# A two-layer hybrid diffusion trunk on one core: mixer parameters loaded at the stage's head, eight modulation halves beside each FFN, all mixer weight splits on VectorE

## The chip, the cores and the metric

The kernel runs on one core of a Trainium2 chip. It is one launch. The metric is the device time of the launch in microseconds, as the median of several runs; beside it stands one profiled execution, from which every row below comes. The engines are TensorE (PE; its weight loads are listed apart as PEld), VectorE (DVE), ScalarE (ACT), GpSimd (POOL) and SyncE (SP), which here only issues DMAs.

## What is computed

384 tokens (128 context tokens and 256 latent ones) of width 1024 pass through two layers, all in float32. The reference, cut to what matters here:

```python
def trunk_layer(x, cond, lp, l, cache):
    mod = silu(cond) @ lp['w_ada'] + lp['b_ada']      # w_ada: 1024 x (9*1024), per layer
    mod = mod.reshape(cond.shape[0], 9, 1, 1024)      # nine vectors, for two conds
    h = rms_norm(x, norm_g[0]) * (1 + mod[:, 1]) + mod[:, 0]
    x = x + 0.5 * mod[:, 2] * swiglu(h, w_gate[0], w_up[0], w_down[0])   # 1024 -> 2816 -> 1024
    h = rms_norm(x, norm_g[1]) * (1 + mod[:, 4]) + mod[:, 3]
    x = x + mod[:, 5] * token_mix(h, lp, l, cache)
    h = rms_norm(x, norm_g[2]) * (1 + mod[:, 7]) + mod[:, 6]
    return x + 0.5 * mod[:, 8] * swiglu(h, w_gate[1], w_up[1], w_down[1])

def token_mix(h, lp, l, cache):
    proj = h @ lp['w_in']            # queries, keys, values, gates of four mixers; 4*1024 merge logits
    out_a = gated_delta(...)         # A: DeltaNet, a triangular solve in every chunk of 64
    lam = exp(sum(lam_p[0]*lam_p[1])) - exp(sum(lam_p[2]*lam_p[3])) + lam_init   # da_lambda
    out_b = diff_attention(rope(rms(b_q)), rope(rms(b_k)), b_v, lam)   # B: two softmaxes, lam between
    out_c = mlstm(...)               # C
    out_d = retention(...)           # D, decay from ret_decay_logit
    y = sum(sigmoid(merge_logits[m]) * (out[m] @ lp['w_branch'][m]) for m in range(4))
    return y @ lp['w_out']
```

It also returns the new states of the four mixers and the new keys and values.

## The kernel before

**Layout.** Tokens lie in the free dimension (384 wide), features in eight blocks of 128 partitions. Each weight tile (128x8x128, or 128x2x512 in the down-projections) comes by DMA as `raw` (1 MB, two tiles, three buffers, issued by SP). `split_unit` then makes two parts of it: `whi`, a cast on ScalarE (L168), and `wlo`, the rest, a subtraction on VectorE or GpSimd (L172). There are three buffers of each part. A product takes three matmuls per block: L185, L186 (both with `whi`) and L187 (with `wlo`).

**Stages.** Each layer runs FFN1 (`ffn`: 22 gate and up tiles, then the down-projection in two halves `dg` of 11 splits each), a norm, `mixers`, a norm, and FFN2. In `mixers` the branches come in the order retention, mLSTM, DeltaNet's first part, attention, DeltaNet's last part; `merge` computes gates (`mg`, branches 3, 2, 1, 0) and branch products (`pb`) and is interleaved with attention and DeltaNet. DeltaNet's solve is a chain of 31 rows in turn on VectorE (the `aR` loop: multiply L1335, reduce L1337, each row longer than the one before).

**Order.** A scheduler with a cost model sets the order of the instructions of every engine. The order is fixed when the kernel is built; at run time each engine works its own list from the top and waits on semaphores. A tile that waits for a buffer, or a VectorE instruction that waits for a DMA, holds all that stands behind it on its engine.

**Modulation vectors.** A vector `mod` of a layer is a product of two conditions with 1024x1024 of `w_ada`. It is made in one of two ways. On TensorE (`ada`): two halves, each with 16 matmul records that write `arow` (L261), then four small transposes `acol` (L271). On VectorE (`ada_beside`): per half four loads `braw` of 512 KB (two buffers, L300) and 20 VectorE instructions, two scalings (L315), 14 multiply-adds (L317), two transposes (L323) and two reductions (L324); a generator hands them out in steps of two instructions, ten steps per half, one step after each split that VectorE does in `ffn`. At the end of an FFN the rest of the generator is run out.

**Splits in `mixers`.** In the projections the second tile of each load is split on GpSimd (`lo_eng`), and so are the gates and branch weights of branches 3, 2 and 1 (`POOLM`). With ten others (units 2 and 3 after a norm) these are 98 splits on GpSimd. GpSimd also adds the branch results to `y` (L1487).

**Small parameters.** The gate biases `gb`, `al`, the decay logits `lg`, the rotary table `rope`, the norm weights `bgn` and the `da_lambda` product `blp` are loaded where they are used. `blp` (L1109) is issued at the head of attention, its first VectorE instruction is L1112; `nlam` and `rg` follow from these.

Of the kernel before, what the change touches and what calls it, by code (L numbers as in the profile page):

```python
# [8 lines left out]
F32 = mybir.dt.float32  # L9
# [32 lines left out]
POOLM = (3, 2, 1)  # L42
# [74 lines left out]
class Trunk:  # L117
# [431 lines left out]
    def ffn_body(self, l, i, jobs, beside, nxt):  # L549
# [40 lines left out]
        for dg in range(2):  # L590
            acc = [self.mmps(name="pd") for _ in range(4)]
            units = []
            for f in range(0, KF, 4):
# [4 lines left out]
                for q in range(0, nf, 2):  # L598
                    w = split(raw[:, q:q + 2], [128, 2, 512])
# [115 lines left out]
    def gate_stage(self, l, keep, p):  # L715
# [3 lines left out]
        gb = p.tile([128, 4, 8], F32, tag="gb", name="gb")  # L719
        nc.vector.memset(gb[:, 0], 0.0)  # L720
        al = p.tile([128, 8], F32, tag="al", name="al")
        for dst, nm in ((gb[:, 1], "dn_dt_bias"), (gb[:, 2], "ml_i_bias"), (gb[:, 3], "ml_f_bias"), (al, "dn_a_log")):
            nc.sync.dma_start(dst, I[nm][l].rearrange("d h -> (d h)").unsqueeze(0).to_broadcast([128, 8]))
# [17 lines left out]
        nc.scalar.activation(out=al, in_=al, func=AF.Exp)  # L741
# [115 lines left out]
    def mix_ret(self, l, p):  # L857
        nc, I = self.nc, self.I
        lg = p.tile([128, 12], F32, name="lg")
        nc.sync.dma_start(lg[:, 0:8], I["ret_decay_logit"][l].rearrange("d h -> (d h)").unsqueeze(0).to_broadcast([128, 8]))  # L860
        nc.vector.tensor_copy(lg[:, 8:12], self.prm[l][:, R_RT:R_RT + 4])
        nc.vector.tensor_scalar_mul(lg, lg, -1.0)
        self.softplus(lg, [128, 12])
        nc.vector.tensor_scalar_mul(lg, lg, -1.0)
# [226 lines left out]
    def mix_attn(self, l, p):  # L1091
        nc, I = self.nc, self.I
        lam0 = 0.8 - 0.6 * math.exp(-0.3 * l)
        rope = p.tile([128, 2, 2, 32], F32, name="rope")
        nc.sync.dma_start(rope, I["rope"])
        gn = p.tile([128, 2, 32], F32, name="bgn")
        nc.sync.dma_start(gn[:, 0], I["da_qn_g"][l:l + 1].to_broadcast([128, 32]))
        nc.sync.dma_start(gn[:, 1], I["da_kn_g"][l:l + 1].to_broadcast([128, 32]))

        rg = p.tile([128, 2, 2, 2, 32], F32, name="brg")  # L1100
        for b in range(2):
            nc.gpsimd.tensor_tensor(rg[:, b, 0], gn, rope[:, b, 0].unsqueeze(1).to_broadcast([128, 2, 32]), op=ALU.mult)
            for a in range(2):
                sv, gv, ov = (t.rearrange("p i (g a e) -> p i g a e", a=2, e=8) for t in (
                    rope[:, b, 1].unsqueeze(1).to_broadcast([128, 2, 32]), gn, rg[:, b, 1]))
                for i in range(2):
                    nc.gpsimd.tensor_tensor(ov[:, i, :, a], gv[:, i, :, 1 - a], sv[:, i, :, a], op=ALU.mult)
# [3 lines left out]
        lam = p.tile([128, 2], F32, name="blam")  # L1111
# [505 lines left out]
```

## Time and profile before

| | |
|---|---|
| median of three runs | 2138.11 us (2131.19 to 2139.86) |
| the profiled execution, its own time | 2140.96 us |
| span of the profile | 2139.2 us |
| mean granted TensorE clock | 0.978 of full speed |
| busy: PE, DVE, ACT, POOL | 96%, 69%, 39%, 22% |

How to read it: the span is what lies between the first and the last recorded instruction; the profiled execution's own time is 1.8 us longer. A stretch of the span, from one time to another, can be asked for each engine's busy time; a busy TensorE is then compared with the length of the stretch. In the lists of instructions a bracket at the end names how long the engine stood idle just before that row, and what ended the idle time. The chain that ended last goes back from the last instruction to what released each one.

### The profile page before, as it was taken

Reading aid. Unit: us, or ns where it says so; the run is one execution under the profiler, and the core shown is the slowest. Engines: PE = TensorE matmul, PEld = TensorE weight load, DVE = VectorE, ACT = ScalarE, POOL = GpSimd, SP = SyncE. Lnnn points to the kernel's source line nnn. Section 1 sums busy time; section 2 is a strip of 40 time slices with the busy share of each in tenths; the row PEclk is TensorE's granted clock in tenths of the full one; section 3 lists DMA queues with packets and bytes.
Section 4 is the critical chain, followed back from the end, with each engine's and each line's share of the span. In section 5 each row is a group of like instructions: output and inputs, shape, how many; then the busy total and the mean of one; then the engine's idle time right before and its main releaser. Section 6 shows DMA issues by size and latency. Waiting matters only on the chain.

```text
span 2139.2 us, 31932 instructions
## 1 busy us (share of the span) xinstructions
PE 2062.1 (96%) x12450; PEld 1992.0 (93%) x12450; DVE 1469.3 (69%) x2716; ACT 842.9 (39%) x1514; POOL 466.2 (22%) x375
## 2 busy tenths in 40 slices
PE   7999999988899999999999999999888999999999
PEld 5889999888789999999999999999877999999999
DVE  4867678678955578776778776678699445795433
ACT  3533335453343245333344332363533423463322
POOL 3000014434354252000120000243243722500000
PEclk8999999999899999999999999999998999999999
DMA  9775545434142355565467554444332423454432
GB/s 312 266 266 171 172 139 173 132 97 121 52 123 70 111 187 171 185 186 178 148 221 260 169 177 168 144 127 138 99 99 77 116 72 129 148 167 128 135 123 79
DMA packets 280566, 322.75 MB, mean 151 GB/s; under 512 B 42784, under 2 KB 214368, under 8 KB 280160
## 3 DMA queue, kind: packets, MB, share of 16 engines
q1 hardware_dynamic: 280144, 320.46, 47.7%
q8 instruction: 98, 1.61, 0.3%
q14 instruction: 52, 0.43, 0.1%
q10 hardware_dynamic: 272, 0.26, 0.0%
HBM read 313.00 MB, written 7.69 MB: 150 GB/s over the span
## 4 chain that ended last, share of the span: by engine, by line
PE 83%; DVE 13%; DMA 2%; ACT 1%; issue 1%; SPq 0%; DVEq 0%; ACTq 0%
PE pg L185 6%; PE pd L185 6%; PE pg L186 6%; PE pd L186 6%; PE pd L187 6%; PE pg L187 6%; PE pu L187 6%; PE pu L185 6%; PE pu L186 6%; PE mg L187 3%; PE mg L185 3%; PE mg L186 3%; DVE aR L1335 2%; PE mm L185 1%; PE mm L186 1%; PE mx L1389 1%
## 5 line engine op out<-in xcount | busy, mean ns | idle before, releaser
L168 ACT CAST whi<-raw 128x1024 fp32r<-128x1024 f32 x422 | 442.6, 1050 | 880.8 <-PE pd L186 212.9
L172 DVE TENSOR_TENSOR wlo<-raw,whi 128x1024 fp32r<-128x1024 f32 x324 | 401.3, 1239 | 304.1 <-ACT whi L168 298.8
L172 POOL TENSOR_TENSOR wlo<-raw,whi 128x1024 fp32r<-128x1024 f32 x98 | 246.4, 2518 | 331.6 <-ACT whi L168 304.9
L386 POOL TENSOR_SCALAR xg<-xT,gs 128x128 f32<-128x128 f32 (+1 forms) x96 | 92.8, 982 | 798.3 <-DVE xT L538 775.7
L185 PE MATMUL pd<-hh,whi 128*128 128x384 f32 x704 | 237.6, 337 | 0.0
L186 PE MATMUL pd<-hl,whi 128*128 128x384 f32 x704 | 237.3, 337 | 0.0
L187 PE MATMUL pd<-hh,wlo 128*128 128x384 f32 x704 | 234.8, 337 | 0.0
L317 DVE SCALAR_TENSOR_TENSOR acc<-braw,cond,acc 128x512 f32<-128x512 f32 x280 | 198.7, 749 | 0.2 <-DMA braw<-in_w_ada 0.2
L185 PE MATMUL pg<-hhi,whi 128*128 128x384 f32 x536 | 180.2, 336 | 0.0
L186 PE MATMUL pg<-hlo,whi 128*128 128x384 f32 x536 | 179.4, 335 | 0.0
L187 PE MATMUL pg<-hhi,wlo 128*128 128x384 f32 x536 | 179.3, 334 | 0.0
L185 PE MATMUL pu<-hhi,whi 128*128 128x384 f32 x536 | 179.1, 334 | 0.0
L187 PE MATMUL pu<-hhi,wlo 128*128 128x384 f32 x536 | 179.1, 334 | 0.0
L186 PE MATMUL pu<-hlo,whi 128*128 128x384 f32 x536 | 179.1, 334 | 0.0
L185 PE MATMUL mg<-hhi,whi 128*128 128x384 f32 x512 | 178.0, 348 | 0.0
L186 PE MATMUL mg<-hlo,whi 128*128 128x384 f32 x512 | 177.3, 346 | 0.0
L187 PE MATMUL mg<-hhi,wlo 128*128 128x384 f32 x512 | 175.5, 344 | 0.9 <-DVE wlo L172 0.9
L186 PEld LDWEIGHTS pd<-hl,whi 128*128 128x128 f32 x704 | 132.3, 188 | 0.1
L185 PEld LDWEIGHTS pd<-hh,whi 128*128 128x128 f32 x704 | 132.3, 188 | 0.1
L187 PEld LDWEIGHTS pd<-hh,wlo 128*128 128x128 f32 x704 | 132.1, 188 | 0.0
L185 PEld LDWEIGHTS pg<-hhi,whi 128*128 128x128 f32 x536 | 100.6, 188 | 3.6 <-ACT hh L581 3.4
L186 PEld LDWEIGHTS pg<-hlo,whi 128*128 128x128 f32 x536 | 100.7, 188 | 1.7 <-issue 1.7
(417 smaller groups left out, 4629.5 us busy)
## 6 DMA issues: line engine op xcount, KB each, us to landing
raw<-in_w_in SPq DMA_DIRECT2D x62, 1024.0 KB
raw<-in_ffn_w_gate SPq DMA_DIRECT2D x44, 1024.0 KB
raw<-in_ffn_w_up SPq DMA_DIRECT2D x44, 1024.0 KB
braw<-in_w_ada SPq DMA_DIRECT2D x80, 512.0 KB
raw<-in_ffn_w_down SPq DMA_DIRECT2D x40, 1024.0 KB
araw<-in_w_ada SPq DMA_DIRECT2D x32, 1024.0 KB
raw<-in_w_branch SPq DMA_DIRECT2D x16, 512.0 KB
raw<-in_w_out SPq DMA_DIRECT2D x8, 1024.0 KB
```

What stands on the lines that cost most here:

```text
L168: nc.scalar.copy(hi, src)
L172: self.last_split = (eng or nc.vector).tensor_tensor(lo, src, hi.bitcast(F32), op=ALU.subtract)
L185: nc.tensor.matmul(ps, w[0], x[0], start=start, stop=False)
L186: nc.tensor.matmul(ps, w[0], x[1], start=False, stop=False)
L187: self.last_mm = nc.tensor.matmul(ps, w[1], x[0], start=False, stop=stop)
L317: nc.vector.scalar_tensor_tensor(acc[s], raw[:, g], c, acc[s], op0=ALU.mult, op1=ALU.add)
L386: self.nc.gpsimd.tensor_scalar(xg[kk][:, a:e], self.xT[:, kk, a:e], gs[:, s, kk:kk + 1], None, op0=ALU.mult)
L1335: nc.vector.tensor_tensor(pr, X[:, 0:r, 0:r].rearrange("p k c -> p c k"), M[:, r, 0:r].unsqueeze(1).to_broadcast([112, r, r]), op=ALU.mult)
L1389: nc.tensor.matmul(ps[:, 64 * h:64 * h + 64], Z[d][:, b, h], x[:, 64 * h:64 * h + 64], start=(h == 0), stop=(h == 3))
```

## The change

It does three things.

1. Each of the FFNs (layer, i) = (0,0), (0,1) and (1,0) has eight halves of modulation vectors beside it, where it had six; vectors 4 of layer 0 and 3 and 4 of layer 1 go from `ada` to `ada_beside`. A split in the down-projection hands out two steps where it handed out one.
2. `mixer_parameters`, called first in `mixers`, loads and computes the small parameters. They live in the stage's pool, `blp` and `rope` in the ring of temporaries.
3. `lo_eng` and `POOLM` are gone: 88 of the 98 splits on GpSimd go to VectorE, 44 in each layer.

```diff
-POOLM = (3, 2, 1)
...
-        def split(src, shape):
+        def split(src, shape, n=1):
             w = self.split_unit(src, shape)
             if self.last_split.ins.engine == mybir.EngineType.DVE:
                 with self.after(self.last_split):
-                    next(beside, None)
+                    for _ in range(n):
+                        next(beside, None)
             return w
...
-                    w = split(raw[:, q:q + 2], [128, 2, 512])
+                    w = split(raw[:, q:q + 2], [128, 2, 512], 2)
...
-    def lo_eng(self, m):
-        return self.nc.gpsimd if m else self.nc.vector
...
-            w = self.split_unit(raw[:, :, 128 * m:128 * m + 128], [128, KD, 128], self.lo_eng(m))
+            w = self.split_unit(raw[:, :, 128 * m:128 * m + 128], [128, KD, 128])
...
-        lp = p.tmp([128, 2, 2, 32], "blp")
-        nc.sync.dma_start(lp, I["da_lambda"][l].rearrange("a d -> (a d)").unsqueeze(0).to_broadcast([128, 128]).rearrange(
-            "p (a b d) -> p a b d", a=2, b=2))
...
-            eng = nc.gpsimd if m in POOLM else nc.vector
...
-            w = self.split_unit(cur["g"][:, :, 128 * q:128 * q + 128], [128, KD, 128], eng)
+            w = self.split_unit(cur["g"][:, :, 128 * q:128 * q + 128], [128, KD, 128])
...
+    def mixer_parameters(self, l):
...
+        lp = self.ring.tmp([128, 2, 2, 32], "blp")
+        lam = bp.tile([128, 4], F32, name="blam", bufs=1)
+        rope = self.ring.tmp([128, 2, 2, 32], "rope")
...
+        for dst, nm in ((self.gb[:, 1], "dn_dt_bias"), (self.gb[:, 2], "ml_i_bias"), (self.gb[:, 3], "ml_f_bias"),
+                        (self.al, "dn_a_log"), (self.lg[:, 0:8], "ret_decay_logit")):
+            nc.sync.dma_start(dst, I[nm][l].rearrange("d h -> (d h)").unsqueeze(0).to_broadcast([128, 8]))
...
     def mixers(self, l):
         nc = self.nc
         with self.pool("bp") as self.bp:
+            self.mixer_parameters(l)
             xs = self.dr.tile([128, KD, T], F32, tag="xs", name="xs", bufs=1)
...
-                mods = {(0, 0): (0, (2, 3, 4)), (0, 1): (0, (8,)), (1, 0): (1, (3, 4)), (1, 1): None}
-                slow = {(0, 0): ((0, 5), (0, 6), (0, 7)), (0, 1): ((1, 0), (1, 1), (1, 2)), (1, 0): ((1, 5), (1, 6), (1, 7)),
-                        (1, 1): ((1, 8),)}
+                mods = {(0, 0): (0, (2, 3)), (0, 1): (0, (8,))}
+                slow = {(0, 0): ((0, m) for m in (4, 5, 6, 7)), (0, 1): ((1, m) for m in (0, 1, 2, 3)),
+                        (1, 0): ((1, m) for m in (4, 5, 6, 7)), (1, 1): ((1, 8),)}
```

What stands where, as the two builds give it. Lines of the kernel after are those of its own file.

VectorE in the down-projection of FFN1 of layer 0, before (`braw`, `acc`, `cond`: load, sum and condition of a modulation half):

```order
L172 TENSOR_TENSOR wlo<-raw,whi 128x1024
L317 SCALAR_TENSOR_TENSOR acc<-braw,cond,acc 128x512 x2
L172 TENSOR_TENSOR wlo<-raw,whi 128x1024
L317 SCALAR_TENSOR_TENSOR acc<-braw,cond,acc 128x512 x2
L172 TENSOR_TENSOR wlo<-raw,whi 128x1024
L317 SCALAR_TENSOR_TENSOR acc<-braw,cond,acc 128x512 x2
```

The same place after:

```order
L171 TENSOR_TENSOR wlo<-raw,whi 128x1024
L316 SCALAR_TENSOR_TENSOR acc<-braw,cond,acc 128x512 x4
L171 TENSOR_TENSOR wlo<-raw,whi 128x1024
L316 SCALAR_TENSOR_TENSOR acc<-braw,cond,acc 128x512 x4
L171 TENSOR_TENSOR wlo<-raw,whi 128x1024
```

Between two splits there are four instructions of the modulation halves where there were two.

SP at the head of attention of layer 0, before (`out_new_mlstm` are stores of mLSTM's final state, `bck` the cached keys, `raw` the next weights):

```order
L1085 DMA out_new_mlstm_C<-cso 64x2x64
L1086 DMA out_new_mlstm_n<-cso 64x2x1
L1095 DMA rope<-in_rope 128x128
L1097 DMA bgn<-in_da_qn_g 128x32
L1098 DMA bgn<-in_da_kn_g 128x32
L1109 DMA blp<-in_da_lambda 128x128
L1124 DMA bck<-in_cache_diff_k 128x4x64
L177 DMA raw<-in_w_in 128x8x256
```

After, `blp` and `rope` stand among the first weights of FFN1 of layer 0:

```order
L176 DMA raw<-in_ffn_w_gate 128x8x256
L1484 DMA blp<-in_da_lambda 128x128
L299 DMA braw<-in_w_ada 128x2x512
L1488 DMA rope<-in_rope 128x128
L176 DMA raw<-in_ffn_w_up 128x8x256
```

And the others stand behind the store `xs` at the head of `mixers` (before, `gb`, `al` and `lg` stood ahead of it, right behind the last `raw` of FFN1):

```order
L1515 DMA xs<-xT 128x3072
L1483 DMA gb<-in_dn_dt_bias 128x8
L1483 DMA gb<-in_ml_i_bias 128x8
L1483 DMA gb<-in_ml_f_bias 128x8
L1483 DMA al<-in_dn_a_log 128x8
L1483 DMA lg<-in_ret_decay_logit 128x8
```

So two loads moved far ahead of their use, and the others moved behind a store that waits for FFN1's result.

VectorE near the end of DeltaNet's solve in layer 0, before (`bmx`, `bsum`, `brc`, `be` belong to attention's softmax, `y` and `mgs` to the merge):

```order
L1335 TENSOR_TENSOR aR<-aR 112x784
L1337 TENSOR_REDUCE aR<-aR 112x28
L1193 RECIPROCAL brc<-bsum 128x2
L1335 TENSOR_TENSOR aR<-aR 112x841
L1194 SCALAR_TENSOR_TENSOR bsum<-brc,bnlam,bsum 128x1
L1485 SCALAR_TENSOR_TENSOR y<-mgs,pb 128x384
L1337 TENSOR_REDUCE aR<-aR 112x29
```

The same two rows of the solve after:

```order
L171 TENSOR_TENSOR wlo<-raw,whi 128x1024
L1297 TENSOR_TENSOR aR<-aR 112x784
L1155 RECIPROCAL brc<-bsum 128x2
L1299 TENSOR_REDUCE aR<-aR 112x28
L1156 SCALAR_TENSOR_TENSOR bsum<-brc,blam,bsum 128x1
L1445 SCALAR_TENSOR_TENSOR mgs<-mgs,pb 128x384
L1297 TENSOR_TENSOR aR<-aR 112x841
L1157 SCALAR_TENSOR_TENSOR be<-be,bsum 128x384
L171 TENSOR_TENSOR wlo<-raw,whi 128x1024
L1299 TENSOR_REDUCE aR<-aR 112x29
```

From the first L1335 to the last of a layer, VectorE's list had 102 instructions with no split in layer 0 and 98 in layer 1; it now has 128 and 124, with 11 splits each. The merge is further on at the same point: when DeltaNet's last transposes (L673) come on TensorE, 744 of its 768 gate matmuls and 144 branch matmuls stand ahead of them, where 685 and 130 did.

## Rows read from the trace of the kernel before

**Rows 1.** The page: engines' busy time, the chain by engine, splits on GpSimd.

```profile
PE 2062.1 (96%) x12450; PEld 1992.0 (93%) x12450; DVE 1469.3 (69%) x2716; ACT 842.9 (39%) x1514; POOL 466.2 (22%) x375
...
PE 83%; DVE 13%; DMA 2%; ACT 1%; issue 1%; SPq 0%; DVEq 0%; ACTq 0%
...
L172 POOL TENSOR_TENSOR wlo<-raw,whi 128x1024 fp32r<-128x1024 f32 x98 | 246.4, 2518 | 331.6 <-ACT whi L168 304.9
```

**Rows 2.** Stretches of the span, busy time and count of each engine, granted clock.

```profile
core 0: us, PE busy (x) PEld busy (x) DVE busy (x) ACT busy (x) POOL busy (x), PEclk, DMA share, GB/s
...
240.00:337.00 97.00, 97.00 (x572) 96.43 (x571) 68.78 (x108) 33.50 (x44) 17.80 (x23) 1.00 0.53 167
...
460.00:490.00 30.00, 19.17 (x110) 18.85 (x108) 15.78 (x39) 16.82 (x43) 6.40 (x4) 0.80 0.39 87
...
535.00:600.00 65.00, 53.29 (x264) 46.14 (x264) 63.34 (x108) 23.30 (x55) 21.21 (x8) 0.88 0.24 72
600.00:740.00 140.00, 139.19 (x929) 137.07 (x928) 69.34 (x136) 44.53 (x98) 58.31 (x31) 0.98 0.32 95
...
1099.00:1290.00 191.00, 191.00 (x1132) 183.59 (x1132) 146.97 (x235) 77.43 (x126) 2.91 (x2) 1.00 0.63 202
...
1510.00:1530.00 20.00, 12.95 (x73) 12.74 (x72) 11.70 (x31) 12.00 (x28) 4.77 (x2) 0.90 0.33 75
...
1580.00:1660.00 80.00, 67.43 (x335) 60.71 (x336) 74.07 (x119) 26.87 (x63) 27.47 (x11) 0.85 0.24 71
```

**Rows 3.** TensorE in time order at one modulation half: start, busy, instruction.

```profile
1132.04 0.34 PE L187 MATMUL pu<-xs,wlo 128*128 128x386 f32 x1
1132.31 1.92 PE L261 MATMUL arow<-araw,cond 128*32 128x512 f32 x16
1134.16 0.44 PE L185 MATMUL pu<-xs,whi 128*128 128x386 f32 x1
```

**Rows 4.** VectorE in time order at the `da_lambda` load.

```profile
484.99 0.22 DVE L1112 TENSOR_TENSOR blp<-blp 128x64 f32<-128x64 f32 x1 [9.76 <-DMA blp<-in_da_lambda]
```

**Rows 5.** Who waited for tile `blp`, in both layers: us, times.

```profile
  DMA blp<-in_da_lambda: 17.8, 2
```

**Rows 6.** The chain that ended last, 476 to 486 us: start, length, what.

```profile
476.82 8.14 DMA blp<-in_da_lambda
...
485.88 0.47 PE mx L673
```

**Rows 7.** VectorE, then GpSimd, in time order, 541 to 545 us.

```profile
541.46 2.18 DVE L1335 TENSOR_TENSOR aR<-aR 112x144 f32<-112x144 f32 x1
...
544.36 0.47 DVE L1335 TENSOR_TENSOR aR<-aR 112x169 f32<-112x169 f32 x1
...
541.07 2.38 POOL L172 TENSOR_TENSOR wlo<-raw,whi 128x1024 fp32r<-128x1024 f32 x1 [7.08 <-ACT whi L168]
```

**Rows 8.** Groups of instructions, 535 to 600 us: count, busy and mean, idle before.

```profile
L1335 DVE TENSOR_TENSOR aR<-aR 112x4 f32<-112x4 f32 (+29 forms) x30 | 29.1, 971 | 0.5
...
L172 POOL TENSOR_TENSOR wlo<-raw,whi 128x1024 fp32r<-128x1024 f32 x8 | 22.3, 2800 | 44.8 <-ACT whi L168 44.8
```

**Rows 9.** VectorE, then ScalarE, in time order in the down-projection.

```profile
258.67 1.23 DVE L172 TENSOR_TENSOR wlo<-raw,whi 128x1024 fp32r<-128x1024 f32 x1 [1.61 <-ACT whi L168]
259.81 1.41 DVE L317 SCALAR_TENSOR_TENSOR acc<-braw,cond,acc 128x512 f32<-128x512 f32 x2
262.83 1.22 DVE L172 TENSOR_TENSOR wlo<-raw,whi 128x1024 fp32r<-128x1024 f32 x1 [1.61 <-ACT whi L168]
...
303.35 1.05 ACT L168 CAST whi<-raw 128x1024 fp32r<-128x1024 f32 x1 [3.11 <-PE pd L186]
```

**Rows 10.** VectorE groups by shape, whole span.

```profile
L380 DVE TENSOR_TENSOR sqacc<-sqacc,sqt 128x384 f32<-128x384 f32 x42 | 27.3, 650 | 6.0 <-ACT sqt L379 5.1
...
L406 DVE TENSOR_TENSOR xs<-xg,xs 128x384 fp32r<-128x384 f32 x35 | 23.9, 703 | 5.2 <-ACT xs L405 5.2
...
L538 DVE SCALAR_TENSOR_TENSOR xT<-pd,gt,xT 128x256 f32<-128x256 f32 x32 | 15.2, 476 | 0.0
```

**Rows 11.** DMA, 264 to 272 us, in 40 slices of 0.2 us; what moved.

```profile
GB/s 0 0 0 0 0 20 205 82 31 92 266 307 440 369 440 369 430 379 440 379 440 358 348 277 338 338 389 399 379 164 92 72 21 0 0 0 0 0 0 0
DMA packets 800, 1.57 MB, mean 197 GB/s; under 512 B 32, under 2 KB 32, under 8 KB 800
```

More of the change, by code (lines that the diff above doesn't have):

```diff
@@ L632, in proj_tm @@
         raw = self.wcols(self.I["w_in"][l], c0)
-        w = [self.split_unit(raw[:, 4 * m:4 * m + 4], [128, 4, 256], self.lo_eng(m)) for m in range(2)]
+        w = [self.split_unit(raw[:, 4 * m:4 * m + 4], [128, 4, 256]) for m in range(2)]
         for b in range(3):
@@ L718, in gate_stage @@
         nc.scalar.copy(grow, self.proj_gates(l))
[L719 to L723, printed above, removed]
+        gb, al = self.gb, self.al
         tp = self.mxps([128, 3, 128])
@@ L740, in gate_stage @@
         self.softplus(sp.rearrange("p b a r -> p (b a r)"), [128, 48])
-        nc.scalar.activation(out=al, in_=al, func=AF.Exp)
         nc.vector.scalar_tensor_tensor(sp[:, :, 0], sp[:, :, 0], -1.0, al.unsqueeze(1).to_broadcast([128, 3, 8]),
@@ L858, in mix_ret @@
         nc, I = self.nc, self.I
[L859 to L864, printed above, removed]
+        lg = self.lg
         dm = p.tile([128, 2, 4, 128], F32, name="dm")
@@ L1092, in mix_attn @@
         nc, I = self.nc, self.I
[L1093 to L1107, printed above, removed]
-        lp = p.tmp([128, 2, 2, 32], "blp")
-        nc.sync.dma_start(lp, I["da_lambda"][l].rearrange("a d -> (a d)").unsqueeze(0).to_broadcast([128, 128]).rearrange(
-            "p (a b d) -> p a b d", a=2, b=2))
-        lam = p.tile([128, 2], F32, name="blam")
-        nc.vector.tensor_tensor(lp[:, :, 0], lp[:, :, 0], lp[:, :, 1], op=ALU.mult)
-        nc.vector.tensor_reduce(lam, lp[:, :, 0], axis=AX, op=ALU.add)
-        nc.scalar.activation(out=lam, in_=lam, func=AF.Exp)
-        nlam = p.tile([128, 1], F32, name="bnlam")
-        nc.vector.scalar_tensor_tensor(nlam, lam[:, 1:2], -lam0, lam[:, 0:1], op0=ALU.add, op1=ALU.subtract)
-        gcol = p.tile([128, 1], F32, name="bgc")
-        nc.vector.tensor_scalar_mul(gcol, self.prm[l][:, R_NG + 1:R_NG + 2], 1.0 - lam0)
+        gn, rg, nlam, gcol = self.gn, self.rg, self.nlam, self.gcol
         xt = p.tile([128, 3, 2, 256], F32, name="bx")
@@ L1461, in prepare @@
         def prepare(m, d):
-            eng = nc.gpsimd if m in POOLM else nc.vector
             if d == 0:
@@ L1469, in prepare @@
             if d % 4 == 0:
-                cur["w"] = self.split_unit(cur["raw"].pop(0), [128, 2, 512], eng)
+                cur["w"] = self.split_unit(cur["raw"].pop(0), [128, 2, 512])
         def load(m, d):
@@ L1578, in run @@
                         self.nc.sync.dma_start(self.cst[:, NC1:], self.I["cst2"])
-                mods = {(0, 0): (0, (2, 3, 4)), (0, 1): (0, (8,)), (1, 0): (1, (3, 4)), (1, 1): None}
-                slow = {(0, 0): ((0, 5), (0, 6), (0, 7)), (0, 1): ((1, 0), (1, 1), (1, 2)), (1, 0): ((1, 5), (1, 6), (1, 7)),
-                        (1, 1): ((1, 8),)}
-                jobs = [self.ada(mods[l, i][0], *mods[l, i][1]) if mods[l, i] else iter(()) for i in range(2)]
+                mods = {(0, 0): (0, (2, 3)), (0, 1): (0, (8,))}
+                slow = {(0, 0): ((0, m) for m in (4, 5, 6, 7)), (0, 1): ((1, m) for m in (0, 1, 2, 3)),
+                        (1, 0): ((1, m) for m in (4, 5, 6, 7)), (1, 1): ((1, 8),)}
+                jobs = [self.ada(mods[l, i][0], *mods[l, i][1]) if (l, i) in mods else iter(()) for i in range(2)]
                 beside = [self.ada_beside([(*m, hf) for m in slow[l, i] for hf in range(2)]) for i in range(2)]
```

31 lines of the change are left out of this document (added).

## The prediction

> **What bounds the kernel now.** I read the page first: TensorE is busy 96% of the span and holds 83% of the chain, VectorE holds 13% of it and is busy 69% [rows 1]. So most of the time is matmuls and can only fall if matmuls go or TensorE's gaps do. Second, the stretches, to see where the gaps are [rows 2]. In the down-projection (240 to 337 us) TensorE is busy 97.00 of 97.00 us with 572 matmuls, 0.17 us each; in 1099 to 1290 it is 191 of 191. In the mixers it is not: 460 to 490 has 19.17 of 30, 535 to 600 has 53.29 of 65, and their counterparts in layer 1 have 12.95 of 20 and 67.43 of 80. In those stretches the granted clock is 0.80, 0.88, 0.90 and 0.85 too; elsewhere in the rows it is 0.98 or 1.00. Third, what stood in each gap. In the first it is one DMA: VectorE waits 9.76 us for `blp` [rows 4], 17.8 us over both layers [rows 5], and the chain runs through that load for 8.14 us on its way to the matmul at 485.88 [rows 6]. In the second it is VectorE, busy 63.34 of 65 us [rows 2], most of it the solve, whose L1335 alone takes 29.1 us [rows 8]. Fourth, the order of the two kernels, for who comes behind whom.
>
> **Part 1, modulation on VectorE.** It takes three vectors off TensorE. One half there pushes the next matmul from 1132.04 to 1134.16: 2.12 us where a matmul takes 0.17, so 1.95 [rows 3]. Six halves are 11.7 us. I leave the four small transposes out, since the other way has four small matmuls of its own. The stretches in which they stand are full (191 of 191), so all 11.7 us count: **-11.7**.
>
> The six halves cost VectorE 20 instructions each, 0.7 us by the pair's 1.41 [rows 9]: some 85 us over three FFNs. In the down-projection a split begins every 4.16 us (258.67 to 262.83); of that the split's pitch is 1.14 (258.67 to 259.81), two multiply-adds occupy 1.41 and 1.61 are idle [rows 9]. Four multiply-adds need 2.8, so VectorE is at 1.14 + 2.8 = 3.94 of 4.16: it fits, with about 0.2 left per split. What it can't do is catch up. Where the first half of the output ends, VectorE also has four blocks of residual and norm: 4 x (0.476 + 0.650 + 0.703) = 7.3 us [rows 10]. The delay that a split bears: ScalarE's cast waits for TensorE to free a buffer and then runs 1.05 us [rows 9]; with three buffers the new weights are needed two splits later, 2 x 4.16 = 8.3 us, and cast and split take 1.05 + 1.14, so some 6 us are spare. 7.3 against 6 is 1.3 us late, in three FFNs: **+4**. From below it is 0, if the scheduler's order spreads that work; from above 5 us in each FFN, if all but 2 us of the boundary's work adds to the lag, so 15.
>
> **Part 2, parameters.** The order shows that only `blp` and `rope` go far ahead, into FFN1 of layer 0 and the merge of layer 0. Then the 17.8 us of VectorE's waiting go [rows 5]. Not all is won: the load of the next weights stands two issues behind `blp` before, and what lands next is not shown by any row. Between 0 and -17.8 I take **-13**, nearer the full wait, because the chain itself runs 8.14 us through that one load [rows 6] and TensorE idles 10.8 of the 30 us there [rows 2]. Everything else of the parameters (`gb`, `al`, `lg`, `bgn`) now stands behind the store `xs`, which waits for FFN1's last residual: later than before, not earlier. Queued behind them on SP are the mixers' further weights; and ScalarE's exponential of `al` now stands ahead of its casts. The nearest row for such a load is the 8.14 us of `blp` [rows 6]: if ScalarE waited that long in both layers it would be 16 us, if the weights split before cover it, nothing. The first projections' weights stand ahead of the store in SP's order, so I take **+1** over both layers, 0 to 16.
>
> **Part 3, splits on VectorE.** 88 splits leave GpSimd at 2.5 us each [rows 1] and come to VectorE at 1.14 us of pitch [rows 9]: 100 us more of instructions. What they give back: while GpSimd's split at 541.07 ran (2.38 us), VectorE's L1335 of 144 elements took 2.18 us, and the one of 169 elements at 544.36, with no split beside it, 0.47 [rows 7]. That split thus held VectorE for about 1.7 us, more than the 1.14 that it now costs. It is one row; a split beside which VectorE has nothing to do holds it for 0. Between 0 and 1.7 I take 1.25 as an estimate, near the upper end because VectorE is seldom idle in those stretches [rows 2]. So the exchange is about even in VectorE's time, and it is decided by place.
>
> The Trainium skill, "SBUF — State Buffer", section "SBUF: two separate sides", says that VectorE and GpSimd share a pair of ports that one of them holds for a whole instruction, if the VectorE instruction has two inputs in SBUF and the GpSimd one reads SBUF. The 2.18 us against 0.47 agree [rows 7]; by that rule all of the excess goes with the splits, and by the chain of rows here only as much as the path sees.
>
> The path sees it in the solve. Eight splits on GpSimd stand in 535 to 600 us [rows 8]; at 1.25 us they hold VectorE 10 us. The order puts 11 splits on VectorE there, 11 x 1.14 = 12.5, and some more of the softmax, which only moves. So the solve ends 2 us later after its start, or a little more, but at its end 59 gate matmuls and 14 branch matmuls more are done in each layer: 73 x 0.17 = 12.4 us. TensorE's idle time there is 11.7 us in layer 0 and 12.6 in layer 1 [rows 2], and it would be filled. Best case -24.3, plus what a clock of 1.00 in place of 0.88 and 0.85 gives back of 53.29 and 67.43 busy us (6.4 and 10.1): -41. Worst case +8: the solve longer by 4 a layer with nothing gained behind it, since 600 to 740 is full (139.19 of 140) and the same matmuls are merely done at another time. I take **-10**, half of 2 x (12.4 - 2), because VectorE has no room left in the stretch and one late split stops both it and TensorE.
>
> **The sum.** -11.7 + 4 - 13 + 1 - 10 = -29.7. Against the profiled execution's own 2140.96 us that is 2111.3; it stands 2.85 us over the median of the runs, 2138.11, so 2108.4 beside that.
>
> **The rivals.**
> B, VectorE becomes the bound of attention and solve. It is busy 63.34 of 65 there [rows 2], and gets 11 splits and two more rows of softmax. If L1335's long rows have another cause than the split beside them, they stay, and the 12.5 us add to the solve; and behind it only 24 gate matmuls are left to cover DeltaNet's last part, 4 us, where 83 or 14 us were. Then part 3 is +8 in place of -10 and the sum -11.7: 2126. For it: the full stretch. Against it: rows 7.
> In the Trainium skill, "Perfetto Trace Analysis", section "Optimizing Scalar/DVE Operations", stands the rule that speaks for B: with VectorE saturated, giving work to ScalarE or even GpSimd may make sense, the reverse of part 3. It adds that the shared port may spoil this, and here rows 7 show that it does.
> C, slower: the down-projection waits for `braw`. Each split now consumes one load of 512 KB where it consumed half of one, and there are two buffers, so a load, issued when a buffer comes free, has to land within about a split and the next one's subtraction, 4.16 + 1.14 = 5.3 us. With 1 MB and 512 KB asked for together, 1.57 MB took 5.4 of the 8 us, from slice 6 to slice 33 of 0.2 us [rows 11]. Now 2 MB must pass in two splits, 8.32 us: at the same 290 GB/s 7.2 us. If a load behind a weight tile takes 0.8 us over its 5.3, a VectorE that has only 0.2 us to spare is late by 0.6 in each pair of splits; over 22 splits x 3 FFNs and with the boundary's work on top, 0.8 x 20 x 3 = 48 us at worst in place of the 4: 2152. It decides at a landing time of some 5.5 us; below that it costs nothing.
> D, larger gain: TensorE's idle time in the solve is all filled and the clock stays up, part 3 is -35: 2083.
> E, the parameters do not do it: `blp` is early, but attention's start waits for the next load, and part 2 is +1 only: 2121.
>
> **How the numbers follow.** About 0.5%, 11 us, is what a measurement of this kernel can tell from no change: under 2127 is faster, over 2149 slower. Forecast 2100 to 2120: 0.56. D, 2080 to 2100: 0.13. E, 2116 to 2126: 0.06. B, 2120 to 2134: 0.17, half on each side of 2127. C, over 2140: 0.08, three quarters of it over 2149. Faster: 0.56 + 0.13 + 0.06 + 0.07 = 0.82; slower 0.06; the rest, 0.12, no difference. The range from 2088 to 2133 leaves out C, the last of B and the lower part of D, some 0.17.
>
> **What would show it.** Right: no modulation matmul of vector 4 or 3 on TensorE beyond the ones that stay; no wait for `blp`, with 460 to 490 us at over 25 of 30 busy; L1335 back under 1 us for the shapes that took 2 and 3; the stretch of the solve with TensorE at 60 of 65 or more. Wrong: TensorE under 95% in a down-projection with VectorE waiting for `braw` (C) or splits that end late after the first output half (the +4 mis-sized); a solve over 72 us long with TensorE idle behind it (B); another DMA as the releaser at attention's start (E).

## The result: 2077 us, twice the gain that was forecast

The kernel after takes 2076.84 us (2074.81 to 2079.72, 4 runs) against 2137.02 for the kernel before; the ratio is 0.9723, interval 0.9709 to 0.9738. On a second chip it is 0.9738 (0.9724 to 0.9751). That is 56 to 60 us gained where 29.7 were forecast, and below the range's lower end of 2088. Its profiled execution has a span of 2073.0 us and a mean granted clock of 0.991.

The page after, engines, chain, splits and modulation, beside [rows 1]:

```profile
PE 2031.0 (98%) x12366; PEld 1970.4 (95%) x12366; DVE 1540.2 (74%) x2921; ACT 840.9 (41%) x1511; POOL 268.8 (13%) x287
...
PE 88%; DVE 8%; DMA 1%; issue 1%; ACT 1%; SPq 0%; POOL 0%; DVEq 0%; ACTq 0%; POOLq 0%
...
L171 DVE TENSOR_TENSOR wlo<-raw,whi 128x1024 fp32r<-128x1024 f32 x412 | 506.1, 1229 | 277.9 <-ACT whi L167 276.9
L316 DVE SCALAR_TENSOR_TENSOR acc<-braw,cond,acc 128x512 f32<-128x512 f32 x364 | 256.9, 747 | 3.0 <-DMA braw<-in_w_ada 2.9
```

VectorE does 71 us more and holds 8% of the chain in place of 13%. TensorE's busy time is 31 us lower, and the span is 66 us shorter, so the other 35 are idle time of TensorE that went.

Where they went is read stage by stage. I cut each trace at the first matmul of a down-projection (`pd`), of the mixers' projections (`mm`), of the gates (`mg`) and of the output projection (`wo`), and take the lengths (us; U is everything up to a down-projection, in U3 from the first gate matmul `pg` on, D the down-projection; the number is that of the FFN, counted over both layers). All differences are against the one profile of before, whose run was the longest of its chip.

| | U1 | D1 | projections 0 | merge 0 | U3 | D3 | projections 1 | merge 1 |
|---|---|---|---|---|---|---|---|---|
| before | 240.5 | 92.2 | 190.6 | 254.1 | 195.7 | 91.9 | 184.6 | 253.0 |
| after | 235.7 | 92.3 | 168.8 | 238.2 | 186.7 | 92.3 | 173.5 | 248.4 |
| difference | -4.8 | +0.1 | -21.8 | -16.0 | -9.0 | +0.4 | -11.1 | -4.6 |

The stages left out differ by 0.4 at most. The mixers give 53.5 of 66 us. Their stretches of the kernel before, in order of time (PE, PEld, DVE, ACT, POOL busy, granted clock, DMA share, GB/s):

```profile
332.70:523.30 190.60, 176.09 (x1165) 170.71 (x1157) 144.85 (x397) 93.93 (x206) 74.28 (x78) 0.94 0.41 118
523.30:777.40 254.10, 238.59 (x1455) 228.03 (x1454) 168.52 (x294) 85.58 (x178) 100.02 (x51) 0.96 0.33 98
1381.60:1566.20 184.60, 174.25 (x1156) 168.16 (x1156) 138.94 (x386) 93.76 (x207) 72.57 (x79) 0.97 0.43 124
1566.20:1819.30 253.10, 237.65 (x1456) 228.75 (x1454) 168.50 (x300) 85.13 (x178) 100.61 (x51) 0.95 0.33 97
```

The same four of the kernel after:

```profile
328.00:496.80 168.80, 168.03 (x1161) 163.04 (x1159) 140.98 (x393) 96.67 (x212) 40.32 (x64) 1.00 0.47 135
496.80:735.00 238.20, 233.05 (x1460) 224.24 (x1459) 170.52 (x345) 84.11 (x176) 32.02 (x22) 0.99 0.36 104
1331.10:1504.60 173.50, 171.83 (x1152) 165.70 (x1152) 139.38 (x387) 94.82 (x207) 39.87 (x63) 0.98 0.45 131
1504.60:1753.00 248.40, 237.18 (x1460) 225.96 (x1459) 171.29 (x344) 85.30 (x177) 30.90 (x21) 0.98 0.34 99
```

Two things are to be seen. TensorE's idle time (length less busy) falls from 55.8 to 18.8 us, 13.7 of it in the first projections, which now have 168.03 of 168.80 busy. And the same matmuls take less: 16.5 us less over the four stretches, as the granted clock goes from 0.94 to 1.00 in the first and from 0.95 to 0.97 up to 0.98 and 0.99 in the others. In these stretches taken together TensorE's gaps thus cost more than their length. How that looks is seen at the gap of [rows 4] in the kernel before: TensorE stands idle from about 475 to 485.88 us, and from 480 to 490 the granted clock is 0.50, the lower of its two levels (1.2 GHz).

```profile
470.00:480.00 10.00, 5.04 (x30) 4.72 (x28) 4.92 (x16) 7.36 (x15) 2.34 (x1) 0.91 0.12 20
480.00:490.00 10.00, 4.12 (x20) 4.13 (x20) 4.91 (x11) 0.59 (x1) 1.65 (x2) 0.50 0.59 150
```

VectorE's busy time in these stretches hardly grew, though 88 splits came to it (44 of some 1.2 us a layer). The reason is in the durations. If one adds up by how much each VectorE instruction is longer than the lower quartile of its own shape (leaving out what is under 0.15 us), the four stretches before give 27 + 40 + 25 + 36 = 128 us, those after 13 + 3 + 11 + 4 = 31 (the sums move by some 3 us with how one tells shapes apart).

### The profile page after: what moved, and what is told of

It reads as the page before. It is cut to its first block, busy times and chain, and to the rows that moved or that the text cites. A ratio compares the mean times of both kernels' runs of the same rounds, so it can differ in the third digit from the quotient of the medians.

```text
span 2073.0 us, 31895 instructions
## 1 busy us (share of the span) xinstructions
PE 2031.0 (98%) x12366; PEld 1970.4 (95%) x12366; DVE 1540.2 (74%) x2921; ACT 840.9 (41%) x1511; POOL 268.8 (13%) x287
## 4 chain that ended last, share of the span: by engine, by line
PE 88%; DVE 8%; DMA 1%; issue 1%; ACT 1%; SPq 0%; POOL 0%; DVEq 0%; ACTq 0%; POOLq 0%
PE pg L184 6%; PE pg L185 6%; PE pg L186 6%; PE pu L184 6%; PE pu L186 6%; PE pu L185 6%; PE pd L184 6%; PE pd L185 6%; PE pd L186 6%; PE mg L186 3%; PE mg L184 3%; PE mg L185 3%; PE mm L186 3%; PE mm L185 3%; PE mm L184 3%; DVE wlo L171 2%
## 5 line engine op out<-in xcount | busy, mean ns | idle before, releaser
L171 DVE TENSOR_TENSOR wlo<-raw,whi 128x1024 fp32r<-128x1024 f32 x412 | 506.1, 1229 | 277.9 <-ACT whi L167 276.9
L316 DVE SCALAR_TENSOR_TENSOR acc<-braw,cond,acc 128x512 f32<-128x512 f32 x364 | 256.9, 747 | 3.0 <-DMA braw<-in_w_ada 2.9
L385 POOL TENSOR_SCALAR xg<-xT,gs 128x128 f32<-128x128 f32 (+1 forms) x96 | 99.9, 1056 | 784.0 <-DVE xT L537 758.6
L184 PE MATMUL mg<-hhi,whi 128*128 128x384 f32 x512 | 177.0, 346 | 1.4 <-ACT mgs L1419 1.3
L1447 POOL TENSOR_TENSOR y<-y,mgs 128x384 f32<-128x384 f32 x48 | 69.9, 1468 | 429.5 <-DVE mgs L1445 412.7
L186 PEld LDWEIGHTS mg<-hhi,wlo 128*128 128x128 f32 x512 | 98.2, 192 | 13.3 <-DVE wlo L171 12.1
L184 PEld LDWEIGHTS mg<-hhi,whi 128*128 128x128 f32 x512 | 98.3, 192 | 4.2 <-ACT mgs L1419 1.7
```

Source lines behind the costliest of these rows:

```text
L171: self.last_split = (eng or nc.vector).tensor_tensor(lo, src, hi.bitcast(F32), op=ALU.subtract)
L184: nc.tensor.matmul(ps, w[0], x[0], start=start, stop=False)
L186: self.last_mm = nc.tensor.matmul(ps, w[1], x[0], start=False, stop=stop)
L316: nc.vector.scalar_tensor_tensor(acc[s], raw[:, g], c, acc[s], op0=ALU.mult, op1=ALU.add)
L385: self.nc.gpsimd.tensor_scalar(xg[kk][:, a:e], self.xT[:, kk, a:e], gs[:, s, kk:kk + 1], None, op0=ALU.mult)
L1447: nc.gpsimd.tensor_tensor(y[:, d], y[:, d], s, op=ALU.add)
```

## The parts one at a time

Kernels of this section are the kernel before with one part of the change, or the kernel after with one part taken back. The first is part 1 alone:

```diff
...
-                    w = split(raw[:, q:q + 2], [128, 2, 512])
+                    w = split(raw[:, q:q + 2], [128, 2, 512], 2)
...
+                mods = {(0, 0): (0, (2, 3)), (0, 1): (0, (8,))}
...
```

> The kernel before with part 1 alone: eight halves beside three FFNs, two steps per split in the down-projection. Both theories: 11 to 14 us faster (2123 to 2126), since six halves of 1.95 us leave a full TensorE and the trace of the kernel after shows its FFN up-projections 4.8 and 9.0 us shorter and its down-projections 0.1 to 0.4 us longer.

Measured: 0.9966 (0.9954 to 0.9978), 7 us, below the expected 11 to 14. In its trace U1 is 5.0 and U3 9.0 us shorter and the three down-projections 0.9 longer together, as in the kernel after. That is 13 us by these stages and 7 by the medians. The kernel before ran a little faster on that chip (2132 us) than its profile shows, but no profile of it was taken there, so where the other 6 us are is not shown. The mechanism stands, and of the stages U3 is the sure one: between two profiles of the kernel after U3 differs by less than 0.1 us, U1 by 2.7 (235.7 and 238.4).

Part 2 alone (`mixer_parameters` and what it replaces; here only its call):

```diff
...
+            self.mixer_parameters(l)
...
```

> The kernel before with part 2 alone: mixer_parameters at the head of the stage. Theory 1 (the wait for blp costs its idle time and, behind it, TensorE's lower granted clock): 25 to 32 us faster (2105 to 2112). Rival (it costs only the wait, and the rest of the gain in the mixers comes from the splits): 10 to 17 us faster (2120 to 2127).

Measured: 1.001 (0.9999 to 1.0022). Neither: it gains nothing. Its profile does not say so everywhere: its projections take 178.7 and 183.7 us and its merges 255.1 and 256.2, so beside the one profile of before the first projections are 11.9 us shorter. What those of before take in its usual runs on that chip was not profiled, so this stays open.

Part 3 alone:

```diff
...
-            w = self.split_unit(raw[:, :, 128 * m:128 * m + 128], [128, KD, 128], self.lo_eng(m))
+            w = self.split_unit(raw[:, :, 128 * m:128 * m + 128], [128, KD, 128])
...
-            eng = nc.gpsimd if m in POOLM else nc.vector
...
```

> The kernel before with part 3 alone: all mixer splits on VectorE. Theory 1: 15 to 22 us faster (2115 to 2122). Rival (the splits on GpSimd hold VectorE all through the mixers, and the projections feel it too): 33 to 40 us faster (2097 to 2104).

Measured: 0.9902 (0.9886 to 0.9918), 21 us.

The kernel after without part 2 (again only the call):

```diff
...
-            self.mixer_parameters(l)
...
```

> The kernel after without part 2. If the parts add up, it is slower than the kernel after by what part 2 alone gains: theory 1 25 to 32 us (2102 to 2109), rival 10 to 17 us (2087 to 2094). A larger loss than part 2 alone gains would say that the wait for blp is worth more once the splits are out of the way.

Measured: 0.9847 (0.9830 to 0.9863), so part 2 is worth 0.011 to 0.0124, 23 to 26 us, here. With the splits on VectorE, what the wait for `blp` holds is seen in that trace. VectorE in time order, and then what TensorE waited for from 460 to 480 us:

```profile
474.19 0.23 DVE L1109 TENSOR_TENSOR blp<-blp 128x64 f32<-128x64 f32 x1 [9.64 <-DMA blp<-in_da_lambda]
...
474.95 1.22 DVE L171 TENSOR_TENSOR wlo<-raw,whi 128x1024 fp32r<-128x1024 f32 x1
```

```profile
PE mm L637 <- DVE wlo L171: 8.9, 1, 8.9
```

A split is queued behind the waiting instruction, and TensorE waits 8.9 us for it; in layer 1 it is 7.8. By stages the kernel after is 13.4 and 3.5 us shorter in the projections and 7.0 in merge 0.

The kernel after without part 3, parts 1 and 2 together:

```diff
...
+POOLM = (3, 2, 1)
...
+    def lo_eng(self, m):
+        return self.nc.gpsimd if m else self.nc.vector
...
```

> The kernel after without part 3, so parts 1 and 2 together: the GpSimd splits are back. If part 2 gives nothing as long as GpSimd splits, as alone: 5 to 10 us faster than before (ratio 0.9950 to 0.9975). If part 2's gain only needs part 1: 25 us or more faster (below 0.9885).

Measured: 0.9976 (0.9965 to 0.9988). Part 2 gives nothing as long as GpSimd splits, with part 1 or without. So part 3 is worth 50 us or more behind parts 1 and 2, and 21 alone. Neither of the two has a price of its own: with both undone 0, part 2 alone 0, part 3 alone 21, both together some 50. By stages, in kernels that all have part 1 (us, one profile each):

| | projections 0 | merge 0 | projections 1 | merge 1 |
|---|---|---|---|---|
| part 1 (e1) | 189.3 | 250.6 | 185.2 | 252.8 |
| parts 1 and 2 (e5) | 188.4 | 251.0 | 184.1 | 256.6 |
| parts 1 and 3 (e4) | 182.2 | 245.2 | 177.0 | 246.7 |
| all three (after) | 168.8 | 238.2 | 173.5 | 248.4 |

In the projections part 2 alone gives 2.0 us, part 3 alone 15.3, both 32.2.

Then part 3 was cut in two. The projections' splits back on GpSimd, by the trace 14 a layer:

```diff
...
+            w = self.split_unit(raw[:, :, 128 * m:128 * m + 128], [128, KD, 128], self.lo_eng(m))
...
```

> The kernel after with only the projections' second tiles back on GpSimd (15 splits a layer), the merge's stay on VectorE. Theory (each GpSimd split holds VectorE, and with the wait for blp gone the projections are where it shows): slower than the kernel after by 15 to 25 us, in the projection stage. Rival (only the solve's stretch matters, as the prediction had it): within 6 us of the kernel after.

Measured: 0.9849 (0.9829 to 0.9869), 24 to 27 us slower than the kernel after by the ratios. Its projections take 187.9 and 186.9 us, as before or longer, its merges are the short ones (239.3 and 240.3). The merge's splits back, by the trace 30 a layer:

```diff
...
+            eng = nc.gpsimd if m in POOLM else nc.vector
...
```

> The kernel after with the splits of branches 3, 2 and 1 in the merge back on GpSimd (29 a layer), the projections' stay on VectorE. If the halves add up (e5 lost 50 us for both, e6 24 for the projections): 20 to 30 us slower than the kernel after. If the merge's half is what the prediction had, 10 us: 5 to 14 slower.

Measured: 0.9868 (0.9854 to 0.9881), 28 us slower than the kernel after on the same chip. Here the projections are as short as after (167.1 and 172.2) and the merges 260.0 and 260.8. So in the totals the halves of part 3 add up, 24 to 27 and 28 against some 50. By stages they do not add so neatly: the projections' half costs 32.6 us in the projections, of which 7.0 come back in the merges (merge 1 is 8.1 shorter than in the kernel after), and the merge's half costs 34.2 in the merges.

One thing blurs these differences. Every edit gives VectorE and TensorE another order, and merges change in length that no edit touched: in ten profiles of kernels whose merge splits are all on VectorE, with no extra work on GpSimd (those above and below, the repeated kernel after among them), merge 0 takes 238.2 to 247.3 us and merge 1 240.3 to 250.8. The repeated kernel after has 238.6 and 246.9. So 7 to 9 us of a difference in a merge can be the order alone; no run here separates that from what a part does. The projections bear the argument better: part 2 pays there, and mostly once their splits are on VectorE.

Why it needs that is in the trace without the projections' half. What TensorE waited for, from 330 to 518 us; VectorE and GpSimd in time order ahead of the first wait:

```profile
PE mx L743 <- DVE sp L739: 6.3, 1, 6.3
PE mx L673 <- DVE co L666: 4.0, 1, 4.0
```

```profile
362.83 2.31 DVE L692 TENSOR_SCALAR lz<-se 128x48 f32<-128x48 f32 x1
365.06 3.10 DVE L869 TENSOR_SCALAR kd<-lg,cst 128x4 f32<-128x4 f32 x2
...
362.41 2.69 POOL L171 TENSOR_TENSOR wlo<-raw,whi 128x1024 fp32r<-128x1024 f32 x1 [7.65 <-ACT whi L167]
365.06 2.14 POOL L859 TENSOR_TENSOR dm<-dm,cst 128x512 f32<-128x512 f32 x2
```

The same instruction of the kernel after:

```profile
363.01 0.17 DVE L689 TENSOR_SCALAR lz<-se 128x48 f32<-128x48 f32 x1
```

The wait for `blp` is gone there, but on VectorE's way to the gates `lz` takes 2.31 us beside one split of GpSimd, and the two `kd` behind it 3.10 beside GpSimd's `dm`, which GpSimd makes in every kernel here (in the kernel after a `kd` takes 0.22). TensorE waits 6.3 and 4.0 us in the place of `blp`; in e5 it is 6.4 and 3.8. In the trace of e2, where GpSimd splits too, `lz` takes 0.18 us and the first projections are the shorter ones, 178.7 us; so whether a split meets the chain looks like a matter of the order. That a part of this chain, the softplus of `lg`, was itself moved ahead by part 2 fits with it, but was not tried alone in this setting.

Which of the parameters matter: `gb`, `al` and `lg` loaded and computed where they were, only `blp`, `rope` and `bgn` first:

```diff
...
-        gb, al = self.gb, self.al
...
+        for dst, nm in ((gb[:, 1], "dn_dt_bias"), (gb[:, 2], "ml_i_bias"), (gb[:, 3], "ml_f_bias"), (al, "dn_a_log")):
+            nc.sync.dma_start(dst, I[nm][l].rearrange("d h -> (d h)").unsqueeze(0).to_broadcast([128, 8]))
...
-        lg = self.lg
...
```

> The kernel after, but of the parameters only blp, rope, bgn and what follows from them are in mixer_parameters; gb, al and lg are loaded and computed where they were before. Theory (the gain of part 2 is the load of blp alone): ratio to before as the kernel after, 0.971 to 0.976. Rival (the others being first matters too): over 0.980. If the others first even cost something: under 0.969.

Measured: 0.9759 (0.9744 to 0.9773), on the edge of the first reading: 19 us of part 2's 23 to 26 by the ratios. Its projections (170.8 and 170.7) sum as in the kernel after; what is missing lies in the merge of layer 0 (247.1), where the parameters have nothing to do. I take it for the order that the scheduler happens to give (278 of VectorE's 2921 instructions stand elsewhere in it than in the kernel after); that is not shown by a run of its own.

## Is it GpSimd's reading, or the late split?

A split on GpSimd could cost time because it holds VectorE, or because its result comes 1.3 us later. Two kernels tell these apart. In both, the kernel after gets extra work on GpSimd that no engine waits for, into the half of a raw tile that has been used. By the traces there are 78 extra subtractions (199.8 us of GpSimd) in the one, and 234 fills (224.0 us) and 54 copies of one column in the other. The orders of the two differ little: 26 of 2921 instructions on VectorE and 68 of 12366 on TensorE stand elsewhere. Either differs more from the kernel after (218 and 226 on VectorE), so the two are compared with each other first.

```diff
+    def extra(self, dead, live, w, n):
...
+        for _ in range(n):
+            nc.gpsimd.tensor_tensor(dead, live, w[1].bitcast(F32), op=ALU.subtract)
...
```

> The kernel after, and beside it GpSimd repeats subtractions of the splits' form (SBUF read twice, 2.4 us each) into weight memory that is no longer used, 38 in each layer's mixers; no other engine waits for a result of it. If GpSimd's reading holds VectorE: 20 to 45 us slower than the kernel after. If the splits on GpSimd cost time because wlo came late: within 6 us of it.

```diff
+    def extra(self, dead, live, w, n):
...
+        nc.gpsimd.tensor_copy(dead[:, 0, 0:1], w[1].bitcast(F32)[:, 0, 0:1])
+        for _ in range(3 * n):
+            nc.gpsimd.memset(dead, 0.0)
...
```

> As e7_pool_reads, but in place of each subtraction GpSimd fills the same memory three times (about 2.6 us, nothing read beyond one column). If it is the reading of SBUF that holds VectorE: within 6 us of the kernel after. If any GpSimd work does, or the longer hold on the raw buffers: slower by as much as e7.

Measured: with reads 1.0060 (1.0040 to 1.0081), so the whole gain of the change is lost, some 70 us; with fills 0.9819 (0.9802 to 0.9836), 17 to 20 us slower than the kernel after. So reads cost some 51 us more than fills. The reads go beyond the expected 45. In the solve, VectorE beside two such subtractions, and GpSimd:

```profile
564.39 2.10 DVE L1305 TENSOR_TENSOR aR<-aR 112x169 f32<-112x169 f32 x1
566.52 0.33 DVE L1307 TENSOR_REDUCE aR<-aR 112x13 f32<-112x169 f32 x1
566.88 2.14 DVE L1305 TENSOR_TENSOR aR<-aR 112x196 f32<-112x196 f32 x1
...
563.87 4.86 POOL L177 TENSOR_TENSOR raw<-raw,wlo 128x1024 f32<-128x1024 f32 x2 [11.98 <-DVE wlo L171]
```

The same two rows of the solve beside six fills:

```profile
546.50 0.46 DVE L1306 TENSOR_TENSOR aR<-aR 112x169 f32<-112x169 f32 x1
...
547.36 0.53 DVE L1306 TENSOR_TENSOR aR<-aR 112x196 f32<-112x196 f32 x1
...
546.22 6.02 POOL L178 MEMSET raw<- 128x1024 f32 x6
```

A multiply of 169 elements takes 2.10 us beside a subtraction and 0.46 beside a fill. So it is GpSimd's work that reads which holds such an instruction. Nobody waits for the extra results, so lateness is not needed for the cost; how much a late split adds was not measured.

The expectation for the fills (within 6 us) missed. Nearly all of their 17 to 20 us is in the merge of layer 0 (256.7 us against 238.2). Fills hold another kind of instruction: one with a single tensor input. The softmax's small scaling in the kernel with fills, and in the kernel after (durations in ns: least, median, most):

```profile
L1155 DVE TENSOR_SCALAR bmx<-bmx x24: 148/409/3514, 534.2 to 1639.8; 128x2 f32<-128x2 f32 x24
```

```profile
L1146 DVE TENSOR_SCALAR bmx<-bmx x24: 148/160/681, 520.3 to 1623.9; 128x2 f32<-128x2 f32 x24
```

How much of it is that, how much the longer hold on the raw tiles (which the reads share) and how much another order, was not separated.

## Can more be had?

Four more kernels start from the kernel after. The last ten splits of GpSimd, those behind the norms, to VectorE:

```diff
-        if self.units in (2, 3):
-            eng = nc.gpsimd
```

> The kernel after with the last ten GpSimd splits (those right behind each norm) on VectorE too. If a GpSimd split costs time wherever it stands: 2 to 8 us faster than the kernel after. If VectorE is the later one behind the norm, where it makes the next input: 2 to 10 us slower.

Measured: 0.9883 (0.9868 to 0.9897), 31 us slower than the kernel after, three times the upper end. Behind a norm VectorE is the late engine: TensorE waits for the norm's own small instructions there, which it hardly does in the kernel after (0.3 us in the same stretch). That the splits of 1.1 us ahead of them are what delays them is read from this, not tried by itself. What TensorE waited for from 1040 to 1240 us:

```profile
PE mx L430 <- DVE nr L160: 5.4, 1, 5.4
PE pg L182 <- DVE hn L207: 2.2, 1, 2.2
```

U3 grows by 10.9 us against the kernel after, FFN2's up-projection by 2.9 in layer 0 and 5.6 in layer 1, and the first projections, which follow a norm too, by 5.3 (the second ones are 4.3 shorter). Merge 0 is 8.6 us longer, where none of the ten splits stands; that can be the order. So the rule is not that GpSimd must never split.

The gate splits of the merge first in the order, in both layers:

```diff
...
+            with self.tc.high_priority():
+                w = self.split_unit(cur["g"][:, :, 128 * q:128 * q + 128], [128, KD, 128])
...
```

> The kernel after with the merge's gate splits given high priority in the order. The kernel after still has 2.7 and 7.3 us of TensorE waiting for wlo in its two merges. If these are splits that stand too late on VectorE: 3 to 10 us faster than the kernel after, in the merges. If the solve and the softmax are the later ones: 0 to 10 us slower.

Measured: 0.9757 (0.9741 to 0.9774), 4 to 7 us slower by the ratios, with an interval that overlaps that of the kernel after on the second chip; merge 1 is 3 us shorter and merge 0 7 us longer. The additions to `y` on VectorE:

```diff
-                nc.gpsimd.tensor_tensor(y[:, d], y[:, d], s, op=ALU.add)
+                nc.vector.tensor_tensor(y[:, d], y[:, d], s, op=ALU.add)
```

> The kernel after with the 48 additions to y on VectorE, so that GpSimd reads almost nothing in the merges. If what is left of GpSimd's reading still holds VectorE on the path: 2 to 8 us faster than the kernel after. If VectorE is the bound there: 48 additions of some 0.55 us, up to 26 us slower, more likely 3 to 12.

Measured: 0.9758 (0.9739 to 0.9777), slower by about as much, and as little sure. Merge 0 is 6.6 us longer and merge 1 3.0 shorter, nearly as in e11, where the additions stay on GpSimd; so what they hold or cost by themselves is not shown, but no gain is to be seen.

High priority in layer 1 alone, and the kernel after once more on that chip:

```diff
...
+            with self.tc.high_priority() if l else nullcontext():
...
```

> The kernel after with high priority for the gate splits in layer 1 alone, where e11's merge was 3 us shorter and layer 0's 7 us longer. If that is a property of the order: 2 to 4 us faster than the kernel after. If a merge's length differs so much between orders for other reasons: within 2 us.

> The kernel after itself, for comparison on the same chip: ratio to before 0.971 to 0.974 by all theories.

Measured: 0.9717 (0.9704 to 0.9731), 2072.21 us, against 0.9738 (0.9724 to 0.9751), 2078.22 us. The intervals touch. By the two profiles merge 1 is 1.5 us shorter (245.4 against 246.9); another 2.3 us lie in U1, ahead of any changed instruction. It is the fastest kernel here, by an amount that is not sure.

## Why the prediction fell short

**Part 1, -11.7 and +4.** Right in kind. U1 and U3 give 13.8 us by the profiles (7 in all by the medians of e1); the down-projections cost 0.9 in all, not 4. A split's idle time is what was worked out, some 0.2 us. VectorE in the down-projection after, beside [rows 9]:

```profile
258.03 1.23 DVE L171 TENSOR_TENSOR wlo<-raw,whi 128x1024 fp32r<-128x1024 f32 x1 [0.23 <-ACT whi L167]
259.17 2.73 DVE L316 SCALAR_TENSOR_TENSOR acc<-braw,cond,acc 128x512 f32<-128x512 f32 x4
262.19 1.23 DVE L171 TENSOR_TENSOR wlo<-raw,whi 128x1024 fp32r<-128x1024 f32 x1 [0.28 <-ACT whi L167]
```

The lag behind the first output half was covered after all. Rival C is out: over the whole span VectorE waited for `braw` five times.

```profile
  DVE acc L316: 2.9, 5
```

**Part 2, -13.** The wait went as said; `blp` now holds VectorE once for 2.2 us at 82.7 us, beside [rows 5]:

```profile
  DVE blp L1494: 2.2, 1
```

The number is wrong on both sides: 0 with GpSimd's splits in place (e2, e5), 23 to 26 with them gone (e4). The step that failed is the sum: it took the terms one by one, as if each had its price. While GpSimd splits, another wait can take the place of the first. What TensorE waited for longest in the first projections, in the kernel before and with parts 1 and 2 (e5):

```profile
PE mx L673 <- DVE co L666: 10.8, 1, 10.8
```

```profile
PE mx L744 <- DVE sp L740: 6.4, 1, 6.4
PE mx L674 <- DVE co L667: 3.8, 1, 3.8
```

The bound of -17.8 is not what failed: of the 23 to 26 us 16.9 are in the projections, and 7.0 in merge 0, which is as long in e9 (247.1), where `blp` is loaded early; so those are not shown to be the wait's. The granted clock adds little to this part: from e4 to the kernel after TensorE's busy time falls by 3.6 us in projections 0 (171.60 to 168.03) and rises by 2.8 in projections 1. Of the +1 nothing is to be seen: ScalarE does wait 4.6 us for `al` over both layers, but TensorE's idle time in the two projections is 0.8 and 1.7 us.

**Part 3, -10.** The exchange itself was right: a split on GpSimd holds VectorE for more than it costs there. With the sum over durations it gave 97 us back for 88 splits, 1.1 each, near the 1.25 taken. The step that failed is "the path sees it in the solve". The projections got no term at all, and they hold half of the gain (e6: 24 to 27 us); the merge's half is 28 (e13), not 10. I had looked at the stretches where TensorE idles, and ahead of the wait for `blp` it idled little; I read that as slack of VectorE, and e4 and e6 show that it was not: without GpSimd's splits the projections are 15.3 us shorter with the wait for `blp` still there, and 32.2 without it. The granted clock had no part in the -10; it stood in the best case alone, and TensorE's busy time in the mixers fell by 16.5 us.

In the solve the working held in kind. In layer 0 it is 59.3 us from the start of the first multiply to the start of the last before and 64.0 after, 4.7 more and not 2 (in layer 1 1.0 more), and TensorE is busy 61.80 of that in place of 50.34. The kernel after:

```profile
516.50:580.50 64.00, 61.80 (x349) 55.45 (x348) 63.53 (x128) 26.75 (x61) 5.03 (x2) 0.97 0.34 99
```

The same of the kernel before:

```profile
534.50:593.80 59.30, 50.34 (x253) 44.31 (x254) 58.37 (x102) 19.11 (x45) 19.64 (x7) 0.88 0.25 75
```

The granted clock went from 0.88 to 0.97 with it. One reading was wrong: the 59 gate and 14 branch matmuls that are done earlier are those of layer 0. In layer 1 the kernel before already had 744 and 144 ahead of DeltaNet's last transposes, the kernel after has 768 and 144, so the prediction's 12.4 us are 24 x 0.17 = 4.1 there. Merge 0 is 16.0 us shorter, merge 1 only 4.6. The solve's multiplies and splits after, beside [rows 8]:

```profile
L1297 DVE TENSOR_TENSOR aR<-aR 112x1 f32<-112x1 f32 (+30 forms) x31 | 23.8, 769 | 0.2
...
L171 DVE TENSOR_TENSOR wlo<-raw,whi 128x1024 fp32r<-128x1024 f32 x11 | 13.4, 1220 | 0.0
```

VectorE is full there, as rival B said, and yet the merges do not get longer. No multiply takes over 2.0 us, where three of layer 0 took 2.2 to 3.2 and four of layer 1 2.7 to 3.6. So of the two readings beside which the Trainium skill was named, "SBUF — State Buffer", section "SBUF: two separate sides", is the one that the runs bear out, also in that it is a GpSimd instruction which reads that holds a two-input VectorE instruction (2.10 us, against 0.46 beside a fill).

**Rivals.** D (2083) had the right sign of the error, with the wrong place for most of it: the merges give 20.6 of the mixers' 53.5 us. E, another wait in place of `blp`, is what happens when GpSimd splits (6.3 and 4.0 us for `sp` and `co`), but it is VectorE, not a DMA. In the chances half of B's 0.17 is 0.085 and not 0.07, which changes nothing that follows.

## What to carry to other kernels

When two hindrances stand in the same stage, price the edits together: here one alone gave nothing, the other 21 us, and both some 50. Where every edit gives a new order, look at the stages too: here a merge moved by 7 to 9 us with edits that did not touch it. A wait that ends last hides the slack of everything before it, so ask of each engine in that stage what would end last without it. And read the durations of an instruction beside those of the same shape elsewhere: a VectorE instruction of 0.46 us that takes 2.10 is a wait that no list of waits shows.

## What the runs showed of the hardware

GpSimd's fills, which read nothing, leave VectorE's two-input instructions nearly alone (0.46 and 0.53 us beside six of them) but hold single-input ones. Counted where no other GpSimd instruction overlaps, and long meaning over 0.3 us more than the lower quartile of the same line and shape: beside the fills 2 of 255 two-input instructions are long, 12 of 23 scalings by a scalar and 7 of 22 copies; beside the extra subtractions 44 of 115 two-input instructions, 2 of 10 scalings and 1 of 12 copies. Beside the splits of the kernel before it is 41 of 135 two-input instructions and 10 of 17 scalings, so work of GpSimd that reads can hold both kinds. No reduction is long beside any of the three (60, 32 and 41 of them).

And the granted clock of a stretch of 170 to 190 us went from 0.94 to 1.00 when some 14 us of TensorE's idle time in it went, with which the same matmuls took 8 us less (projections 0). In projections 1 8.7 us of idle time and 2.4 us of matmul time went, from 0.97 to 0.98.
